# A hybrid decoder layer on one core: the Up projection's seven operands made ahead and kept in DRAM, and the last output projection moved to the channel mixer's entry

## The chip, the cores and the metric

The kernel runs on one core of one Trainium2 chip. The metric is the device time of one execution in microseconds (us). The engines are TensorE (PE in the rows, with PEld for its weight loads), VectorE (DVE), ScalarE (ACT) and GpSimd (POOL); SyncE (SP) issues nearly all transfers, in the order in which they stand in its program.

## The reference

One layer, 2048 tokens, model width 1024. The first half is the mixer, the second the channel mixer:

```python
h = modulate(x, norm_mix_g, sh_m, sc_m)
proj = h @ w_in
y = concat(gla_group(proj[:, :GLA_COLS]), rwkv7_group(proj[:, GLA_COLS:]))
x = x + gt_m * (y @ w_out)

h = modulate(x, norm_ffn_g, sh_f, sc_f)
u = h @ ffn_up                        # 1024 -> 2 * 2816
u = causal_conv3(u) + conv_b
gate, val = split(u, 2)
x = x + gt_f * ((silu(gate) * val) @ ffn_down)
out = rms_norm(x, final_g)

def modulate(x, g, shift, scale):     # rms_norm, then scale and shift
    return rms_norm(x, g) * (1 + scale) + shift
```

The RWKV group is a scan over tokens, so its blocks follow one another. All of it is float32.

## The kernel before

Tokens lie in 4 blocks of 512 (NB), activations as tiles of 128 features x 512 tokens, 8 tiles to a block (KT). Every large product of float32 is three matmuls of 128x128 by 128x512: operands are split into hi (a cast, ScalarE) and lo (a subtraction, VectorE or GpSimd), and hi*hi, lo*hi and hi*lo are added in PSUM.

Phase 1, the mixer, ends at about 1440 us. It runs GLA and RWKV in 16 quarters of a block (units; `rwkv_s` and what follows) and beside them a filler: the projections of the next block, and in the last block `spare()`, which is `stage_d` (the output projection) of blocks 0 to 2. `stage_d(b)` multiplies the mix of block b, read back from DRAM (`mixd`, mx), with w_out, eight output tiles ft, adds the residual, stores x2d[b] and makes the norm's rn2[b]. The RWKV part of a quarter ends in a chain: L738, L1017, the power L741 on GpSimd, L113, L1019, L1020, L1026, L1027 and the store of the mix, L1028.

Phase 2, the channel mixer, works on two halves e = 0, 1 of two blocks each. Up (class `Up`) treats two blocks x two halves of the 1024 features as a 2x2 matrix and uses seven products in place of eight (Strassen-Winograd): `Up(j, what)`, what = 1 to 7, is one of them for the pair of output tiles j (22 pairs), 12 matmuls (L1249 to L1251). The seven operands are b11, b21, b22 and the sums t1 to t4 of quarters of the modulated x; each has four k tiles, held as hi and lo for a whole half. `operands_a` makes b11 and b21: load x2d, multiply with the norm's row (L1144), add the shift (L1145, L1146). `operands_b` makes the other five, with `whole` (L1164) putting b11 and b21 together again from hi and lo. Weights are loaded into w_st (L1194), combined on GpSimd (L1227 to L1234) and split (L1124, L1125).

The hidden tiles go through the convolution and the gate (`conv`, `hidden`, in a background list bg, one piece per slot) and then, in groups of 2 or 4 pairs (kgroups), through Down: 16 slots a group, which load a partial sum acc from DRAM, add (L1306 to L1309) and store it.

Half 0 begins with the operands, made before `run`. Half 1 needs block 3, whose mix is the last that phase 1 stores. Its output projection `stage_d(NBLK - 1)` stands at the seam, with the operands of half 1, ahead of the last Down group of half 0 (d_begin, d_step, d_end). `run` goes through a list of slots; it asks for the loads of 6 slots ahead and prepares (splits) 3 ahead. The order within each engine's program is decided by a scheduler from these calls' order and priorities.

## Time and profile before

| | |
|---|---|
| three runs | 2959.83, 2950.89, 2960.01 us; median 2959.83 |
| profiled execution | 2950.25 us, its span 2948.5 us |
| TensorE, VectorE, ScalarE, GpSimd busy | 94%, 75%, 48%, 40% of the span |
| granted clock of TensorE, mean | 0.96 |

The span is the time from the first to the last instruction of the core; some 2 us lie around it. The busy shares are means over stages that differ: TensorE is near full over most of the span and has a few stretches with gaps. The profiled execution is at the lower edge of the three runs.

### The profile page before, as it was taken

To read this page: it belongs to the slowest core of one execution; us is meant where nothing else is said; L and a number is where in the kernel's file an instruction comes from. 1 tells how busy PE (TensorE), PEld (TensorE's weight loads), DVE (VectorE), ACT (ScalarE), POOL (GpSimd) and SP (SyncE) were. 2 spreads that over 40 slices of the span, in tenths; PEclk is the share of its full clock that TensorE was granted. 3 is DMA by queue.
4 is the path that set the end of the run, shared out by engine and by line. 5 is a ranking of instruction groups with operands and counts; after the bars stand their busy time and mean duration, and the time that the engine had idled before them with its cause. 6 is when DMAs were issued, how large, how long until landed. Compare 5 with 4: busy or idle time off the path is not lost.

```text
span 2948.5 us, 54765 instructions
## 1 busy us (share of the span) xinstructions
PE 2764.5 (94%) x20296; PEld 2231.9 (76%) x20296; DVE 2198.3 (75%) x4229; ACT 1407.2 (48%) x2909; POOL 1189.5 (40%) x1212
## 2 busy tenths in 40 slices
PE   6998899999999999899869999999998999999998
PEld 5777777877777777777658788888776788888887
DVE  7368787777877677888587775866879786685867
ACT  4555445445554565555444353533545453353443
POOL 5224232323222233334455463544537454363541
PEclk9999999999989999989979999999998999999999
DMA  8556544544333334533415334243465534425243
GB/s 282 173 166 190 159 122 136 151 143 120 113 112 101 109 115 148 148 101 105 151 53 164 116 104 153 91 138 125 147 200 171 193 101 139 129 97 161 85 132 109
DMA packets 316875, 401.95 MB, mean 136 GB/s; under 512 B 75584, under 2 KB 148544, under 8 KB 316608
## 3 DMA queue, kind: packets, MB, share of 16 engines
q1 hardware_dynamic: 316608, 398.45, 43.2%
q8 instruction: 160, 2.62, 0.4%
q14 instruction: 107, 0.88, 0.1%
HBM read 293.49 MB, written 104.86 MB: 135 GB/s over the span
## 4 chain that ended last, share of the span: by engine, by line
PE 60%; DVE 15%; DMA 7%; issue 3%; ACT 2%; POOL 2%; SPq 0%; DVEq 0%; POOLq 0%; ACTq 0%
PE g_bank L1251 9%; PE g_bank L1249 9%; PE g_bank L1250 9%; PE g_bank L1306 5%; PE g_bank L1308 5%; PE g_bank L1307 5%; PE g_bank L263 3%; PE g_bank L265 3%; PE g_bank L264 3%; DMA w_st<-in_ada_t 1%; DVE w_lo L182 1%; PE gl_bank L679 1%; DMA x_k<-in_x 1%; DMA ub<-x 1%; DVE gl_d L652 1%
## 5 line engine op out<-in xcount | busy, mean ns | idle before, releaser
L1249 PE MATMUL g_bank<-h_hi,w_hi 128*128 128x512 f32 x1232 | 488.7, 397 | 29.0 <-ACT h_hi L1124 12.4
L1251 PE MATMUL g_bank<-h_hi,w_lo 128*128 128x512 f32 x1232 | 481.7, 396 | 16.8 <-POOL w_lo L1125 12.3
L1250 PE MATMUL g_bank<-h_lo,w_hi 128*128 128x512 f32 x1232 | 487.7, 396 | 7.7 <-DVE h_lo L1125 4.7
L1124 ACT CAST w_hi<-w_st 128x512 fp32r<-128x512 f32 (+1 forms) x396 | 239.1, 609 | 465.6 <-PE g_bank L1307 342.6
L1309 DVE SCALAR_TENSOR_TENSOR acc<-g_bank,mod,acc 128x512 f32<-128x512 f32 (+1 forms) x200 | 144.9, 729 | 249.5 <-PE g_bank L1308 234.5
L1125 POOL TENSOR_TENSOR w_lo<-w_st,w_hi 128x512 fp32r<-128x512 f32 x154 | 221.5, 1439 | 229.2 <-ACT w_hi L1124 225.5
L263 PE MATMUL g_bank<-h_hi,w_hi 128*128 128x512 f32 x736 | 299.3, 408 | 5.2 <-ACT carry L320 3.8
L265 PE MATMUL g_bank<-h_hi,w_lo 128*128 128x512 f32 x736 | 297.4, 405 | 3.5 <-DVE w_lo L182 3.5
L1249 PEld LDWEIGHTS g_bank<-h_hi,w_hi 128*128 128x128 f32 x1232 | 235.5, 191 | 84.3 <-ACT h_hi L1124 14.7
L264 PE MATMUL g_bank<-h_lo,w_hi 128*128 128x512 f32 x736 | 295.9, 402 | 0.0
L1251 PEld LDWEIGHTS g_bank<-h_hi,w_lo 128*128 128x128 f32 x1232 | 235.7, 191 | 71.6 <-POOL w_lo L1125 17.8
L1250 PEld LDWEIGHTS g_bank<-h_lo,w_hi 128*128 128x128 f32 x1232 | 235.8, 191 | 58.9 <-DVE h_lo L1125 5.7
L1306 PE MATMUL g_bank<-hh,w_hi 128*128 128x512 f32 x640 | 251.5, 395 | 4.7 <-DVE acc L1309 4.6
L1308 PE MATMUL g_bank<-hh,w_lo 128*128 128x512 f32 x640 | 251.5, 395 | 0.0
L1307 PE MATMUL g_bank<-hl,w_hi 128*128 128x512 f32 x640 | 251.4, 395 | 0.0
L179 ACT CAST w_hi<-w_st 128x512 fp32r<-128x512 f32 x272 | 167.6, 619 | 118.8 <-PE g_bank L264 59.9
L182 POOL TENSOR_TENSOR w_lo<-w_st,w_hi 128x512 fp32r<-128x512 f32 x90 | 128.3, 1425 | 228.6 <-ACT w_hi L179 191.5
L1125 DVE TENSOR_TENSOR w_lo<-w_st,w_hi 128x512 fp32r<-128x512 f32 (+1 forms) x242 | 201.1, 831 | 19.4 <-ACT w_hi L1124 19.4
L182 DVE TENSOR_TENSOR w_lo<-w_st,w_hi 128x512 fp32r<-128x512 f32 x182 | 142.2, 782 | 63.6 <-ACT w_hi L179 52.9
L263 PEld LDWEIGHTS g_bank<-h_hi,w_hi 128*128 128x128 f32 x736 | 141.1, 192 | 37.5 <-ACT carry L320 4.8
L265 PEld LDWEIGHTS g_bank<-h_hi,w_lo 128*128 128x128 f32 x736 | 141.1, 192 | 36.1 <-DVE w_lo L182 5.2
L264 PEld LDWEIGHTS g_bank<-h_lo,w_hi 128*128 128x128 f32 x736 | 141.6, 192 | 28.7 <-issue 0.5
(344 smaller groups left out, 6382.1 us busy)
## 6 DMA issues: line engine op xcount, KB each, us to landing
acc<-acc SPq DMA_DIRECT2D x352, 256.0 KB, 3.1
w_st<-in_ffn_up SPq DMA_DIRECT2D x176, 256.0 KB, 3.0
w_st<-in_w_in SPq DMA_DIRECT2D x168, 256.0 KB, 3.0
proj<-ev SPq DMA_DIRECT2D x100, 256.0 KB, 3.0
w_st<-in_ffn_down SPq DMA_DIRECT2D x80, 256.0 KB, 2.7
w_st<-in_ada_t SPq DMA_DIRECT2D x64, 256.0 KB, 3.4
w_st<-in_w_out SPq DMA_DIRECT2D x64, 256.0 KB, 3.1
x_k<-in_x SPq DMA_DIRECT2D x48, 256.0 KB, 3.7
```

The source lines that it names most:

```text
L182: eng.tensor_tensor(out=lo[:, 0:w], in0=t[:, 0:w], in1=hi[:, 0:w].bitcast(F32), op=ALU.subtract)
L263: PE.matmul(out=ps, lhsT=wh, rhs=hi, start=k == 0, stop=False)
L264: PE.matmul(out=ps, lhsT=wh, rhs=lo, start=False, stop=False)
L265: PE.matmul(out=ps, lhsT=wl, rhs=hi, start=False, stop=k == KT - 1)
L1124: A.copy(out=hi, in_=t)
L1125: eng.tensor_tensor(out=lo, in0=t, in1=hi.bitcast(F32), op=ALU.subtract)
L1249: PE.matmul(out=ps, lhsT=wh[:, c], rhs=hi, start=first and k == 0, stop=False, skip_group_check=True)
L1250: PE.matmul(out=ps, lhsT=wh[:, c], rhs=lo, start=False, stop=False, skip_group_check=True)
L1251: PE.matmul(out=ps, lhsT=wl[:, c], rhs=hi, start=False, stop=last and k == 3, skip_group_check=True)
L1306: PE.matmul(out=ps, lhsT=wh, rhs=hh, start=j == 0, stop=False)
L1307: PE.matmul(out=ps, lhsT=wh, rhs=hl, start=False, stop=False)
L1308: PE.matmul(out=ps, lhsT=wl, rhs=hh, start=False, stop=j == n - 1)
```

## The change

The seven operands of a half are now made whole, in float32, and stored in DRAM (`opd`): `operand_rows` spreads the two norm rows, `operand_a` loads four tiles of x2d, modulates them and stores b11, b21 and b22, `operand_b` makes t1 to t4 of them in place on GpSimd and stores them. For half 0 this is done in phase 1, beside `stage_d(2)`, in memory of its own (pp); for half 1 in the background of half 0, after the Down groups that begin at 2, 6, 10 and 14. Where an operand is needed, `feed` loads it and splits it. The last output projection stands behind the first two units of half 0, its mix in the places of b22 and t4, whose feeds follow it. Both halves are one list of slots; the first two units of half 1 stand ahead of the last Down group of half 0, and the feeds of its operands beside j = 21 and that group.

```diff
+    pp = ph1.enter_context(tc.tile_pool(name="pp", bufs=1))
...
+    NAMES = ("b11", "b21", "t2", "t3", "t1", "b22", "t4")
+    opd = [{n_: [dram.tile([P, NB], F32, name=f"op_{e}_{n_}_{k}") for k in range(4)] for n_ in NAMES} for e in range(NBLK // 2)]
+    def operand_rows(e, r_of):
+        rbs = []
+        for i in range(2):
+            ps = pools["norm"]()
+            for t in range(4):
+                PE.matmul(out=ps[:, t * P:(t + 1) * P], lhsT=rn2[:, 2 * e + i, t:t + 1].broadcast_to([P, P]), rhs=ident, start=True, stop=True)
+            rb = r_of(i)
+            A.copy(out=rb, in_=ps)
+            rbs.append(rb)
+        return rbs
+    def operand_a(e, k, rbs, place):
+        t = {}
+        for n_, i, q in (("b11", 0, k), ("b12", 1, k), ("b22", 1, k + 4), ("b21", 0, k + 4)):
+            xk = place()
+            nc.sync.dma_start(out=xk, in_=x2d[2 * e + i][:, q, :])
+            V.scalar_tensor_tensor(out=xk, in0=xk, scalar=mod[:, 32 + q:33 + q], in1=rbs[i], op0=ALU.mult, op1=ALU.mult)
+            A.activation(out=xk, in_=xk, func=AF.Identity, bias=mod[:, 24 + q:25 + q])
+            if n_ in opd[e]:
+                nc.sync.dma_start(out=opd[e][n_][k], in_=xk)
+            t[n_] = xk
+        return t
+    def operand_b(e, k, t):
+        G.tensor_tensor(out=t["b12"], in0=t["b11"], in1=t["b12"], op=ALU.subtract)
+        G.tensor_tensor(out=t["b22"], in0=t["b12"], in1=t["b22"], op=ALU.add)
+        G.tensor_tensor(out=t["b11"], in0=t["b22"], in1=t["b11"], op=ALU.subtract)
+        G.tensor_tensor(out=t["b21"], in0=t["b22"], in1=t["b21"], op=ALU.subtract)
+        for n_, to in (("b12", "t1"), ("b22", "t2"), ("b11", "t3"), ("b21", "t4")):
+            nc.sync.dma_start(out=opd[e][to][k], in_=t[n_])
...
-            fin = yield from stage_d(b, hd.pop(b), pair=True, before=nxt, after=fin)
+            work = stage_d(b, hd.pop(b), pair=True, before=nxt, after=fin)
+            i = 0
+            while True:
+                try:
+                    next(work)
+                except StopIteration as end:
+                    fin = end.value
+                    break
+                if b == 2:
+                    if i == 0:
+                        rbs = operand_rows(0, lambda j: pp.tile([P, NB], F32, name="op_r", tag=f"r{j}", bufs=1))
+                    elif i < 5:
+                        t = operand_a(0, i - 1, rbs, lambda: pp.tile([P, NB], F32, name="op_x", tag="x", bufs=4))
+                        operand_b(0, i - 1, t)
...
-    def operands_a(b):
...
-    def operands_b(b, hs):
...
+    def feed(e, n_, k, hs):
+        t = ubt()[:, 0:NB]
+        nc.sync.dma_start(out=t, in_=opd[e][n_][k])
+        hi, lo = pair = hc(n_)
+        hs[n_].append(pair)
+        if n_ == "t2":
+            A.activation(out=hi, in_=t, func=AF.Copy, scale=-1.0)
+            V.scalar_tensor_tensor(out=lo, in0=t, scalar=-1.0, in1=hi.bitcast(F32), op0=ALU.mult, op1=ALU.subtract)
+        else:
             split(t, pair, either())
...
+    def feeds(e, names, hs):
+        return [lambda n_=n_, k=k: feed(e, n_, k, hs) for n_ in names for k in range(4)]
...
+    def out_begin():
+        places = iter(["b22"] * 4 + ["t4"] * 4)
+        pools["pair"] = lambda: hc(next(places))
+        out_begin.work = stage_d(NBLK - 1, prep_d(NBLK - 1), lp.tile([P, NB], F32, name="d_ss", tag="cv", bufs=4))
+    def out_step(i, more):
+        next(out_begin.work, None)
+        for p_ in more:
+            p_()
+    def out_end():
+        for _ in out_begin.work:
+            pass
+        bg.extend(feeds(0, ("b22", "t4"), hss[0]))
+    def next_rows():
+        next_rows.rbs = operand_rows(1, lambda j: lp.tile([P, NB], F32, name="op_r", tag="fs", bufs=HB))
+    def next_operand(k):
+        got = {}
+        bg.append(lambda: got.update(operand_a(1, k, next_rows.rbs, acct)))
+        bg.append(lambda: operand_b(1, k, got))
...
+            if e == 0 or j > 0:
+                U(j, 1)
+                U(j, 2)
+            if e == 0 and j == 0:
+                more = feeds(0, ("t2", "t3", "t1"), hss[0])
+                other(out_begin)
+                for i in range(KT):
+                    other(lambda i=i, m=more[i * 3 // 2:(i + 1) * 3 // 2]: out_step(i, m))
+                other(out_end)
             if j > 1 and group_of[j - 2] != group_of[j - 1]:
+                g = group_of[j - 2]
+                slots += down_slots(e, g, hids[e][g])
+                if e == 0 and g[0] == 0:
+                    other(next_rows)
+                elif e == 0 and g[0] <= 14:
+                    other(lambda k=(g[0] - 2) // 4: next_operand(k))
             if j > 0:
                 U(j - 1, 3)
...
+        if more_:
+            unit(1, 0, 1)
+            unit(1, 0, 2)
+            other(flush)
+            other(lambda: bg.extend(feeds(1, ("t2", "t3", "t1", "b22", "t4"), hss[1])))
+            other(lambda: sums[0].extend(lp.tile([P, NB], F32, name="x_ss", tag="fs", bufs=HB) for _ in range(HB)))
+            rest_ = down_slots(e, last, hids[e][last], sums[0])
+            for i, d_ in enumerate(rest_):
+                slots.append(d_)
+                other(lambda: None)
+            other(flush)
...
+    for p_ in feeds(0, ("b11", "b21"), hss[0]):
+        p_()
...
-    hs, pieces = operands_a(0)
-    for p_ in pieces:
-        p_()
-    for p_ in operands_b(1, hs):
-        p_()
```

The rows that follow are from the programs of the two kernels; the shape is that of the output. Lines of the changed kernel are shifted: its L1262 to L1264 are L1249 to L1251 of before, L1207 is L1194, L1030 is L1028, L743 is L741.

TensorE at the entry, before: the last quarter's small matmuls, and behind them the first units of the Up projection.

```order
L219 MATMUL g_bank<-ones_121,x_ss 128x1 x4
L1006 MATMUL rs_bank<-rw_t,rw_sv 64x64 x8
L1010 MATMUL rs_bank<-rw_rbk,rw_uv 64x64 x8
L232 MATMUL g_bank<-ident,rn_120 128x128 x8
L738 MATMUL rj_bank<-ct,rw_ysq 32x8 x16
L1249 MATMUL g_bank<-h_hi,w_hi 128x512 x2
L1250 MATMUL g_bank<-h_lo,w_hi 128x512
L1251 MATMUL g_bank<-h_hi,w_lo 128x512
```

Of the change, behind the same first two units: L263 to L265 are the last output projection.

```order
L1262 MATMUL g_bank<-h_hi,w_hi 128x512
L1263 MATMUL g_bank<-h_lo,w_hi 128x512
L1264 MATMUL g_bank<-h_hi,w_lo 128x512
L263 MATMUL g_bank<-h_hi,w_hi 128x512 x2
L264 MATMUL g_bank<-h_lo,w_hi 128x512
L265 MATMUL g_bank<-h_hi,w_lo 128x512
```

So between the second and the third product of Up there now stand the 192 matmuls of block 3's output projection, the first of them on mix tiles that are there, the later ones on those that the last store of the mix (L1030) brings.

SP at the entry, before: L1028 stores the mix of the last quarter, L1143 and L1171 load x2d for the operands.

```order
L1194 DMA w_st<-in_ffn_up 128x512 x4
L1143 DMA ub<-x_0_115 128x512 x2
L1171 DMA ub<-x_1_116 128x512 x3
L1194 DMA w_st<-in_ffn_up 128x512
L1028 DMA mix_114<-rw_yq 128x4x128
L1194 DMA w_st<-in_ffn_up 128x512
L1171 DMA ub<-x_1_116 128x512 x3
L1194 DMA w_st<-in_ffn_up 128x512
```

Of the change, from the store of the mix of the last quarter but one: op_x and op_b, op_t are tiles of the operands (the digit behind the letter is the k tile), L1060 and L1070 their stores, L1192 the loads of the feeds, L174 weights of the output projection.

```order
L1030 DMA mix_114<-rw_yq 128x4x128
L174 DMA w_st<-in_w_out 128x512 x5
L1060 DMA op_b_3_694<-op_x 128x512
L1060 DMA op_b_3_678<-op_x 128x512
L1070 DMA op_t_3_690<-op_x 128x512
L464 DMA x_2_117<-xr 128x512 x2
L174 DMA w_st<-in_w_out 128x512
L1070 DMA op_t_3_682<-op_x 128x512
L1070 DMA op_t_3_686<-op_x 128x512
L1070 DMA op_t_3_698<-op_x 128x512
L1192 DMA ub<-op_b_0_671 128x512
L1192 DMA ub<-op_b_1_672 128x512
```

The loads of the feeds stand behind the stores of all operands with k = 3, and the store of the last quarter's mix comes behind 13 of these loads.

GpSimd there, in the change: L1066 to L1068 are the last three differences of k = 3, L1240 and L1242 sums of Up weights, L743 the power of the last quarter.

```order
L1240 TENSOR_TENSOR w_st<-w_st 128x512
L1066 TENSOR_TENSOR op_x<-op_x 128x512
L1242 TENSOR_TENSOR w_st<-w_st 128x512
L1067 TENSOR_TENSOR op_x<-op_x 128x512
L1068 TENSOR_TENSOR op_x<-op_x 128x512
L743 TENSOR_TENSOR hn_rk<-hn_rk,mhalf 128x8
L1181 TENSOR_TENSOR h_lo<-ub,h_hi 128x512 x2
```

Before, no difference stood ahead of that power.

SP in the middle of half 0, in the change, after a Down group: L1338 and L1346 are loads and stores of acc, L1207 loads of weights of the Up projection.

```order
L1056 DMA acc<-x_2_117 128x512
L1070 DMA op_t_0_715<-acc 128x512
L1346 DMA acc_7_18305<-acc 128x512
L1060 DMA op_b_0_719<-acc 128x512
L1338 DMA acc<-acc_0_18290 128x512
L1060 DMA op_b_0_703<-acc 128x512
L1207 DMA w_st<-in_ffn_up 128x512
L1070 DMA op_t_0_707<-acc 128x512
L1338 DMA acc<-acc_0_18298 128x512
L1207 DMA w_st<-in_ffn_up 128x512
```

Before, only the rows of acc and the weights stood here.

## Rows read from the trace of the kernel before

**Rows 1.** Page: span; busy time, share and instructions of each engine:
```profile
span 2948.5 us, 54765 instructions
...
PE 2764.5 (94%) x20296; PEld 2231.9 (76%) x20296; DVE 2198.3 (75%) x4229; ACT 1407.2 (48%) x2909; POOL 1189.5 (40%) x1212
```
**Rows 2.** Windows; engines' busy us (x instructions), PEclk, DMA share, GB/s:
```profile
1460.00:1470.00 10.00, 9.35 (x29) 6.72 (x30) 9.87 (x16) 3.91 (x7) 6.67 (x4) 0.67 0.33 105
1500.00:1510.00 10.00, 0.98 (x3) 0.37 (x2) 9.48 (x10) 4.69 (x8) 6.18 (x6) 0.50 0.09 27
1440.80:1522.90 82.10, 45.52 (x240) 33.20 (x240) 66.32 (x82) 36.75 (x64) 50.69 (x37) 0.71 0.30 96
1850.00:1900.00 50.00, 50.00 (x221) 41.07 (x220) 47.03 (x54) 29.71 (x50) 35.02 (x34) 1.00 0.19 59
```
**Rows 3.** PE lines, 1440.8 to 1522.9: busy, mean ns, idle before:
```profile
L1249 PE MATMUL g_bank<-h_hi,w_hi 128*128 128x512 f32 x28 | 16.2, 585 | 25.2 <-ACT h_hi L1124 12.4 <-ACT h_hi L1145 8.5 <-ACT ub L1258 2.5
```
**Rows 4.** Waits of PE, 1440.8 to 1522.9: total us, times, longest:
```profile
PE g_bank L1249 <- ACT h_hi L1124: 12.4, 4, 5.7
PE g_bank L1249 <- ACT h_hi L1145: 8.5, 2, 5.2
```
**Rows 5.** PE timeline at the entry: start us, us:
```profile
1463.24 0.63 PE L1249 MATMUL g_bank<-h_hi,w_hi 128*128 128x512 f32 x1
1463.67 0.63 PE L1250 MATMUL g_bank<-h_lo,w_hi 128*128 128x512 f32 x1
```
**Rows 6.** Windows at the seam:
```profile
2100.00:2300.00 200.00, 180.99 (x776) 145.26 (x775) 176.20 (x214) 103.89 (x176) 107.98 (x83) 0.95 0.52 169
2305.00:2360.00 55.00, 49.94 (x197) 38.62 (x196) 40.00 (x55) 19.46 (x35) 25.34 (x21) 0.91 0.76 249
```
**Rows 7.** Lines of PE, 2100 to 2400:
```profile
L1251 PE MATMUL g_bank<-h_hi,w_lo 128*128 128x512 f32 x213 | 86.1, 407 | 11.7 <-POOL w_lo L1125 9.6 <-DVE w_lo L1125 2.0
...
L264 PE MATMUL g_bank<-h_lo,w_hi 128*128 128x512 f32 x64 | 24.9, 390 | 0.0
L232 PE MATMUL rj_bank<-ident,rn 128*128 128x128 f32 x24 | 3.2, 274 | 0.0
```
**Rows 8.** Waits of PE, 2100 to 2300 and 2305 to 2360:
```profile
PE g_bank L1251 <- POOL w_lo L1125: 9.1, 2, 8.3
...
PE g_bank L1306 <- DVE acc L1309: 3.7, 1, 3.7
```
**Rows 9.** Window at the end of phase 1:
```profile
1385.00:1445.00 60.00, 57.49 (x662) 46.09 (x660) 29.75 (x69) 25.17 (x58) 19.92 (x19) 1.00 0.45 144
```
**Rows 10.** Lines of POOL, 1385 to 1445:
```profile
L244 POOL TENSOR_TENSOR x_ss<-x_ss,x_sq 128x512 f32<-128x512 f32 x7 | 9.0, 1280 | 20.4 <-ACT x_sq L243 20.4
```
**Rows 11.** DMA issues: xcount, KB each, median us to landing:
```profile
mx<-mix SPq DMA_DIRECT2D x32, 256.0 KB, 3.2
...
mix<-rw_yq SPq DMA_DIRECT2D x16, 256.0 KB, 3.0
```
**Rows 12.** Timeline at the entry, POOL and SP:
```profile
1460.31 2.09 POOL L741 TENSOR_TENSOR hn_rk<-hn_rk,mhalf 128x8 f32<-128x8 f32 x1 [1.37 <-DVE hn_rk L1017]
...
1475.17 0.37 SPq L1028 DMA_DIRECT2D mix<-rw_yq  x1
```
**Rows 13.** Window with Down and Up matmuls in half 0:
```profile
1680.00:1730.00 50.00, 50.00 (x219) 40.66 (x218) 27.25 (x36) 15.84 (x26) 19.53 (x19) 1.00 0.57 173
```
**Rows 14.** Lines of DVE, 2100 to 2300:
```profile
L1125 DVE TENSOR_TENSOR h_lo<-ub,h_hi 128x512 fp32r<-128x512 f32 x14 | 12.8, 929 | 0.7 <-ACT h_hi L1124 0.7
...
L182 DVE TENSOR_TENSOR w_lo<-w_st,w_hi 128x512 fp32r<-128x512 f32 x11 | 9.8, 891 | 0.2 <-ACT w_hi L179 0.2
...
L1144 DVE SCALAR_TENSOR_TENSOR ub<-ub,mod,rbc 128x512 f32<-128x512 f32 x8 | 6.0, 745 | 1.4 <-DMA ub<-x 1.4
...
L1177 DVE TENSOR_TENSOR ub<-ub 128x512 f32<-128x512 f32 x4 | 2.8, 709 | 0.8 <-ACT ub L1173 0.8
```
**Rows 15.** Busiest window of the DMA queues:
```profile
1580.00:1590.00 10.00, 10.00 (x45) 8.09 (x44) 5.14 (x8) 2.44 (x4) 2.83 (x4) 1.00 0.94 318
```

More of the change, by code (lines that the diff above doesn't have):

```diff
@@ new lines, in hybrid_kernel, with other @@
+    hids, sums = {}, [[] for _ in range(NBLK // HB)]
+    last = kgroups[-1]
+    slots = []
+    def other(f):
+        slots.append(Other(f))
+    def out_begin():
[10 more added lines that the diff above has]
+        bg.extend(feeds(0, ("b22", "t4"), hss[0]))
@@ L1404, in stage_e @@
                 U(j - 1, 4)
+            if j == NH - 1:
+                step_early(3)
             U(j, 7)
+            if j == NH - 1:
+                step_early()
             U(j, 5)
[L1407 to L1442 removed]
@@ L1443, in stage_e @@
         U(NH - 1, 3)
         U(NH - 1, 4)
-        run(slots)
-        while bg:
-            bg_step()
-        while idle:
-            bg_step()
-        wplace, aplace = iter(["b11"] * 4 + ["b21"] * 4), iter(["t2"] * 4 + ["t3"] * 4)
-        ws, acc = [], [[], []]
-        for ft in range(KT):
-            pair = hc(next(wplace))
-            split(raw(ffn_down[ft][:, k0 * P:k1 * P]), pair, V)
-            ws.append(pair)
-            tag = next(aplace)
-            for i, s_ in enumerate(("hi", "lo")):
-                a_ = h1p.tile([P, NB], F32, name="acc", tag=f"{tag}_{s_}", bufs=4)
-                nc.sync.dma_start(out=a_, in_=accd[bs_[i]][ft])
-                acc[i].append(a_)
@@ L1475, in hybrid_kernel @@
+    for p_ in feeds(0, ("b11", "b21"), hss[0]):
         p_()
     pools["norm"] = lambda: bank("rj")
-    for e in range(NBLK // HB):
-        hs = stage_e(e, hs)
+    run(slots)
+    flush()
+    while idle:
+        bg_step()
+    e = NBLK // HB - 1
+    bs_ = range(e * HB, (e + 1) * HB)
+    k0, k1 = last
+    sums[e].extend(lp.tile([P, NB], F32, name="x_ss", tag="fs", bufs=HB) for _ in bs_)
+    hids, sums, hs = hids[e], sums[e], None
+    wplace, aplace = iter(["b11"] * 4 + ["b21"] * 4), iter(["t2"] * 4 + ["t3"] * 4)
```

135 lines of the change are left out of this document (41 added, 94 removed).

## Prediction

> **What bounds the kernel now.** I read the page first: TensorE is busy for 2764.5 of 2948.5 us [rows 1]. So a change off TensorE's path gains nothing, and one on it can gain at most the 184 us in which TensorE waits. Next I looked for where those are, with the windows of 10 us. Two stretches stand out, and the change touches both.
>
> *The entry of the channel mixer.* The pair of output projections that ends phase 1 is done at 1440.8; from 1523 TensorE runs without a gap. In the 82.1 us between it is busy for 45.5, at a granted clock of 0.71 [rows 2]. What it does there of use is 28 matmuls of each of L1249 to L1251, 84 in all [rows 3]. In steady state 221 such matmuls fill 50 us, 0.226 us each [rows 2]; so these 84 are worth 19.0 us. The other 63 us go to the 156 small matmuls of the RWKV tail and the norms (240 less 84) and, for the most part, to waiting. The waits say to whom: h_hi from ScalarE, 12.4 and 8.5 us [rows 4], that is the hi parts of Strassen operands. They are late because the whole chain that makes them (load, modulate, hi, lo, whole(), differences, split) stands on VectorE in this stretch and VectorE is full (9.48 of 10 us at 1500 to 1510, where TensorE has 0.98 and its granted clock is 0.50) [rows 2]. That is the lower of its two levels, 1.2 GHz of 2.4, and there consecutive matmuls start 0.43 us apart instead of 0.226 [rows 5].
>
> *The seam between the halves*, 2100 to 2400: VectorE is busy for 176.2 of 200 us, TensorE for 181 [rows 6]. In 300 us stand 638 matmuls of the Up projection, 288 of Down, 192 of the last output projection, 1118 in all [rows 7], worth 253 us; the small ones take some 7, of which the spreads L232 are 3.2 [rows 7]. So 40 us are lost here: about 10 of them in the Down group (0,2) of half 1, whose 197 matmuls are worth 45 of 55 us at a DMA share of 0.76 [rows 6] and where TensorE waits for acc [rows 8], and about 30 before it, where it waits for a w_lo that came 8.3 us late [rows 8] behind the operands' work.
>
> **The change at the entry.** Removed there: all of operands_a and operands_b. Added at the end of phase 1: per k tile 4 loads, 4 VectorE multiplies, 4 ScalarE biases, 4 GpSimd differences and 7 stores, 16 + 16 + 16 operations over four k tiles. Over the last 60 us of phase 1 GpSimd is busy for 19.9 and VectorE for 29.8 [rows 9], so 16 x 1.28 [rows 10] = 20 us of GpSimd and 16 x 0.75 (as L1144 has in [rows 14]) = 12 us of VectorE fit beside TensorE's projections, and I cost them at nothing there; if that cover failed, the 20 us of GpSimd would stand at the entry. Added at the entry: 28 feeds, each one load, one cast, one subtraction. And the last output projection, 192 matmuls, moves from the seam to this place.
>
> When can it start? The order has the last RWKV quarter, then the 24 matmuls of U(0,0,1) and U(0,0,2), then the projection on the first four k tiles of ft 0 and 1 (another 24), and only then what needs the last mix. SP has the feeds behind the stores of the k = 3 operands, and these wait for GpSimd, in whose order the last three differences of k = 3 stand just ahead of the power L743 of the last quarter. By rows: a k tile costs a load 3.2 [rows 11], multiply and bias at 0.75, four differences at 1.28 and a store 3.0, some 12 us; the x tiles of k = 3 are loaded when those of k = 2 are stored. I put the last difference at 1461, the first feed's landing at 1465, which is where the first matmuls of the units stood before (1463 [rows 5]). The quarter's tail: before, the power was at 1460.31 and the mix was stored at 1475.17, 14.9 us later [rows 12]. With VectorE freed of operands (9.87 of 10 us in 1460 to 1470 [rows 2]) I give it 12 us from 1461: 1473, and then store and load again, 3.0 + 3.2 [rows 11]: the fifth k tile's matmul at 1483 with what waits in SP between.
>
> From there TensorE has 168 matmuls of the projection and the ready operands t2, t3, t1 ahead of it. Counted at 1523: 48 + (1523 - 1483 - 3)/0.226 = 48 + 163 = 211 matmuls, against 84 before (the 3 us are for the restart at the lower clock). 127 x 0.226 = 28.7 us more work done. From it I take 3 us for b22 and t4, whose places hold the mix until the projection ends, so that their 8 feeds come after it. **Entry: -26 us.** Bounds: if the k = 3 chain is quick and the tail is not held, the start is at 1471: 264 matmuls, -38. If the k = 3 cycle is late by its whole 12 us and SP stands another 5 on the 14 transfers around it (0.82 us each, 256 KB at the 318 GB/s of [rows 15]), the start is at 1500: 136 matmuls, -9.
>
> **In half 0.** After four Down groups the operands of half 1 are made: each place adds 11 transfers, 4 VectorE multiplies, 4 biases, 4 differences. TensorE is at 50 of 50 us with VectorE at 47 [rows 2], so nothing is certain to hide them; but those rows are between Down groups, and the Down groups, where the places are, have VectorE at 27 of 50 [rows 13]. Bounds: nothing, and 4 places x 4 us of VectorE = 16 us. I take **+4 us**, near the lower end by the rows of the Down groups.
>
> **At the seam.** Removed from VectorE in 2100 to 2300: the output projection's and the operands' rows, from the 9.8 us of w_lo L182 to the 2.8 of L1177, eleven kinds with 72 us together, h_lo L1125 the largest [rows 14]. Added: 28 feeds, some 20 of them on VectorE at 0.93 us as h_lo has [rows 14], 19 us. The 192 matmuls leave. That removes the work behind which w_lo was late. What stays: the group (0,2) of half 1, 10 us. What is new: 20 feeds and the b22/t4 pair come in during the last Down group of half 0, which has 16 slots of 12 matmuls, 43 us, with VectorE also adding acc and squares; its 20 + 32 + 8 transfers of 256 KB are 15.7 MB, 49 us at the 318 GB/s of the busiest window [rows 15]. So transfers alone are a little over the matmuls: of the 30 us I take 14 as lost again there, half-way between the ends. **Seam: -16 us.** Bounds: -28 (2 of the 30 stay), -5 (the feeds come nearly as late as the operands did).
>
> Sum: 2950.25 - 26 + 4 - 16 = 2912 us against the profiled execution's own time (span 2948.5, 1.75 around it). The three runs have a median 9.6 us above that; I add a small part of it and say **2914**. A change under 0.3%, about 9 us, is none that a measurement can tell here.
>
> **A rule that speaks against it.** The change adds 112 transfers of 256 KB, 29.4 MB. At 318 GB/s [rows 15] they take 92 us if nothing hides them; in steady state 59 GB/s are moved [rows 2] and beside a Down group 173 [rows 13], so there is room for them, if not at each place. The Trainium skill, "DMA: Bandwidth & Descriptors", section "Where 436 GB/s comes from", puts the limit for a core's share of HBM at about 358 GB/s: by it an estimate of 82 us. The trace agrees so far: its busiest row, 318 GB/s, lies below that.
>
> **Rivals.**
> (a) *The operand chain holds the entry* (0.22): SP's order puts stores that wait for GpSimd ahead of the feeds, and the start is at 1500. Then the entry gives 9, the sum is 2929. For it: all loads and stores go through this one queue. Against it: GpSimd is idle for two thirds of the stretch in which it has to make k = 0 to 2 [rows 9].
> (b) *The seam gives nothing* (0.15): 20 feeds beside the last Down group in one queue cost what the operands did; 5 us instead of 16: 2923; with (a) 2940.
> (c) *Everything is at its good end* (0.15): -38, 0, -28: 2884.
> (d) *Slower* (0.07): in half 0 the weights of the Up projection (w_st) stand in SP's queue behind stores of b21 and t3 that wait for ScalarE and GpSimd. A unit's weights are asked for 6 slots ahead, 6 x 2.7 = 16 us of cover; a k tile's cycle of some 12 us plus its 11 transfers at 0.82 (9 us) is 21. If the cover is used up by acc traffic, each of four places loses up to 15 us: with (a) at the entry and the seam at 5, 2950 - 9 - 5 + 60 = 2996. It decides when a place loses more than 10 us (4 x 10 = the gain forecast). Against it: the rows of Down groups have TensorE at 50 of 50 at a DMA share of 0.57 [rows 13].
> (e) *Transfers are the bound* (0.02): all 92 us show, 2950 - 42 + 92 = 3000. Against it: the rates of [rows 2, 13].
> My forecast, a gain of 30 to 50, has 0.39.
>
> **How the numbers follow.** The likeliest is 2914; (c) and most of (a) and (b) are inside 2886 to 2944, and a little over 0.1 is left out on the upper side, under 0.1 below. Faster by over 0.3% holds in the forecast, (a), (b) and (c) except where (a) and (b) meet: 0.83. Within 0.3%: 0.08. Slower: 0.09, (d) and (e).
>
> **What would show it.** Right: L1249's idle at the entry (its waits for h_hi) falls from 21 to under 10 us; the output projection's matmuls run without gaps from about 1483; the granted clock of 1480 to 1520 is 1.00; VectorE at the seam falls from 88% to about 65%; the wait of 8.3 us for w_lo is gone; in 1600 to 2000 TensorE stays at 50 of 50. Wrong: a gap behind U(0,0,2) that lasts to 1500 and ends on the last mix; TensorE waiting for w_hi or w_lo around a Down group of half 0; a DMA share of 0.9 around 2230 with TensorE waiting for the feeds.

## The result, and the profile after

Five runs of each kernel on one chip: 2974.80 us (2972.22 to 2983.71) after the change, 2950.89 us (2946.09 to 2960.01) before it. The ratio of after to before is 1.0083, with a 95% interval of 1.0064 to 1.0102. The changed kernel is 0.8% slower. I had forecast 2914 us, faster; the range ended at 2944.

The page of the changed kernel (its profiled execution took 2979.16 us):

```profile
span 2977.3 us, 55039 instructions
...
PE 2778.9 (93%) x20296; PEld 2244.9 (75%) x20296; DVE 2163.9 (73%) x4191; ACT 1409.3 (47%) x2925; POOL 1202.0 (40%) x1234
```

Against [rows 1], VectorE has 34 us less to do and the span is 28.8 us longer. Work was removed; the time went into standing. Windows show where. The columns are those of [rows 2]; the first two rows lie in half 0, each just behind a place where operands of half 1 are made, then come the entry and the seam:

```profile
1750.00:1800.00 50.00, 41.73 (x161) 32.59 (x161) 40.25 (x44) 25.52 (x44) 30.22 (x29) 0.90 0.42 131
2000.00:2050.00 50.00, 43.14 (x179) 34.07 (x178) 29.88 (x34) 18.31 (x31) 26.02 (x23) 0.97 0.53 172
...
1440.80:1522.90 82.10, 57.59 (x357) 46.02 (x358) 52.99 (x80) 40.45 (x71) 42.08 (x33) 0.77 0.81 273
1500.00:1510.00 10.00, 10.00 (x38) 8.03 (x38) 8.30 (x11) 6.53 (x11) 4.86 (x4) 0.82 1.00 350
2100.00:2300.00 200.00, 182.01 (x752) 144.31 (x751) 138.09 (x179) 85.04 (x146) 90.70 (x76) 0.95 0.57 183
```

At the entry TensorE starts 357 matmuls where it started 240, and at 1500 to 1510 it is busy for 10.00 us where it had 0.98 [rows 2]: the change does there what it says. At the seam VectorE falls from 176.20 of 200 us [rows 6] to 138.09. But in half 0, where [rows 2] had 221 matmuls in 50 us, there are now stretches with 161 and 179.

**A curve of progress.** To add this up I counted TensorE's large matmuls (128x128 by 128x512, 8720 in each kernel) in order of start and noted when the n-th starts. At one n both kernels have started equally many; those of the last output projection (192) come between n = 2841 and 3045 after the change and between 5505 and 5720 before it, and count as any others. The table is the time in a run's profiled execution less the time at the same n before. Up to n = 2200 every engine has the same program in all of them (the first difference is a load of op_x in SP's, at 1163 us), yet the executions differ there, after the change by 5.2 us (1110.3 and 1115.5); that is no effect of the change, so this lag (last column) is taken off each curve. (With it, the last row is 29.1 us; the spans differ by 28.8.) Three of the four places in which half 1's operands are made lie between n = 3800 and 5330, the fourth between 5500 and 5580, inside the stretch in which the kernel before has its seam.

```
us later than before, from n = 2200
n                          3050    3800    5330    8720 (end)  lag at 2200
after                     -14.2   -12.3   +24.4   +23.9       +5.2
e1 half 1 not made        -15.1   -12.3   -13.4   -30.6       +9.1
e2 half 1 not computed    -16.8   -14.7   -12.5   -26.9       +1.8
e3 other ring             -13.1   -10.1    -1.6   -11.5       +4.7
e4 half 0 not made        -32.0   -29.9    +3.7    +1.2      +12.7
e5 other ring             -14.4   -12.6    -7.7   -22.0       +2.9
e6 other ring             -13.5   -10.4    -4.5   -16.4       +7.1
e7 as e3, earlier         -14.0   -12.2    -6.4   -14.4       +3.7
e8 as e3, k = 3 late       -5.6    -3.9    +2.0    -8.5       +5.3
e9 as e5, norm late       -16.0   -11.9    -9.4   -19.3       +8.2
e10 as e9, earlier        -21.8   -15.0   -12.8   -25.0       +8.2
e11 as e9, on GpSimd      -22.4   -14.8   -13.7   -27.0       +4.5
e12 as e11, order         -22.0   -11.0    -8.4   -23.0       -0.1
```

How far can one such row be read? e3, e5 and e6 came out as one and the same program (see there). Their rows lie 1.3 us apart at n = 3050 (3.7 with those of the changed kernel, e1 and e2, which are the same program up to there too), lose 8.5, 4.9 and 5.9 us over the three places, and end 10.5 us apart. Differences of that size between two rows say nothing.

Row "after" is the whole account. The entry gains 14.2 us where I had 26. Then 1.9 are lost up to n = 3800, in e1 and e4 as well (2.8 and 2.1). The three places lose 36.7: from n = 3900 to 4040 13.3, from 4440 to 4510 10.4, from 4950 to 5030 8.6, the rest between. From n = 5330 on 0.5 is gained, although the fourth place loses 9.4 there, where e1 and e5 gain 2.8; so that place costs 12.2, and without it the seam gives 12.7, where I had 16.

### The profile page after: what moved, and what is told of

The parts are those of the page before. It is cut to its first block, busy times and chain, and to the rows that moved or that the text cites. A ratio compares the mean times of both kernels' runs of the same rounds, so it can differ in the third digit from the quotient of the medians.

```text
span 2977.3 us, 55039 instructions
## 1 busy us (share of the span) xinstructions
PE 2778.9 (93%) x20296; PEld 2244.9 (75%) x20296; DVE 2163.9 (73%) x4191; ACT 1409.3 (47%) x2925; POOL 1202.0 (40%) x1234
## 4 chain that ended last, share of the span: by engine, by line
PE 56%; DVE 14%; DMA 10%; issue 3%; ACT 3%; POOL 2%; SPq 1%; DVEq 0%; POOLq 0%; ACTq 0%
PE g_bank L1264 8%; PE g_bank L1262 8%; PE g_bank L1263 8%; PE g_bank L1319 5%; PE g_bank L1321 4%; PE g_bank L1320 4%; DMA acc<-acc 2%; PE g_bank L263 2%; PE g_bank L265 2%; PE g_bank L264 2%; DMA acc<-x 1%; DMA w_st<-in_ada_t 1%; PE gl_bank L681 1%; DVE w_lo L182 1%; DVE rw_pr L884 1%
## 5 line engine op out<-in xcount | busy, mean ns | idle before, releaser
L1262 PE MATMUL g_bank<-h_hi,w_hi 128*128 128x512 f32 x1232 | 488.6, 397 | 20.6 <-ACT ub L1271 10.7
L1264 PE MATMUL g_bank<-h_hi,w_lo 128*128 128x512 f32 x1232 | 484.1, 397 | 24.5 <-DVE w_lo L1181 17.5
L1322 DVE SCALAR_TENSOR_TENSOR acc<-g_bank,mod,acc 128x512 f32<-128x512 f32 (+1 forms) x200 | 144.5, 728 | 229.7 <-PE g_bank L1321 211.9
L263 PE MATMUL g_bank<-h_hi,w_hi 128*128 128x512 f32 x736 | 300.5, 410 | 7.1 <-ACT carry L320 3.9
L265 PE MATMUL g_bank<-h_hi,w_lo 128*128 128x512 f32 x736 | 298.6, 406 | 0.0
L1264 PEld LDWEIGHTS g_bank<-h_hi,w_lo 128*128 128x128 f32 x1232 | 235.5, 191 | 81.7 <-DVE w_lo L1181 21.9
L1262 PEld LDWEIGHTS g_bank<-h_hi,w_hi 128*128 128x128 f32 x1232 | 236.1, 192 | 75.6 <-ACT ub L1271 14.1
L263 PEld LDWEIGHTS g_bank<-h_hi,w_hi 128*128 128x128 f32 x736 | 142.0, 193 | 39.5 <-ACT carry L320 4.9
L265 PEld LDWEIGHTS g_bank<-h_hi,w_lo 128*128 128x128 f32 x736 | 142.0, 193 | 30.9 <-issue 0.2
```

The costliest lines, as they stand in the source:

```text
L263: PE.matmul(out=ps, lhsT=wh, rhs=hi, start=k == 0, stop=False)
L265: PE.matmul(out=ps, lhsT=wl, rhs=hi, start=False, stop=k == KT - 1)
L1262: PE.matmul(out=ps, lhsT=wh[:, c], rhs=hi, start=first and k == 0, stop=False, skip_group_check=True)
L1264: PE.matmul(out=ps, lhsT=wl[:, c], rhs=hi, start=False, stop=last and k == 3, skip_group_check=True)
```

## The experiments

My first theory: tiles of the new background work (L1056 to L1070) come from acct(), the ring of 5 buffers that Down uses for its partial sums, so a load of x2d can't be issued before a store of acc has landed; the engines, which run in order, stand on the tile. The rivals: the stores in SP's queue, with w_st behind them (rival (d)); the transfers as such (rival (e)); the arithmetic.

**e1, half 1's operands not made.** 2928.61 us, ratio 0.9894 [0.9870, 0.9919].

```diff
-        nc.sync.dma_start(out=t, in_=opd[e][n_][k])
+        nc.sync.dma_start(out=t, in_=opd[0][n_][k])
...
-                elif e == 0 and g[0] <= 14:
+                elif False:
```

> Leaves out the making of half 1's operands in half 0 (its feeds load those of half 0). Theory A (the four places in half 0 cost the time: VectorE and ScalarE stand in order on tiles whose loads wait for a buffer of the acc ring) and theory B (the 44 transfers and SP's queue cost it) both expect that the jumps of some 10 us at each of the four places in the progress of TensorE's large matmuls vanish: 35 to 45 us less, a time of 2930 to 2942. If the single list of slots or the feeds cost the time, it stays at 2970 to 2978.

From n = 3800 to 5330 it loses nothing (-1.1), and from there it gains 17.2. So the whole loss in half 0 comes from making half 1's operands there, and without it the change would gain 1.1%; that is an upper end, since e1 leaves needed work out.

**e2, loads and stores of half 1's operands without the arithmetic.** Same places, same queue, same ring, same bytes. 2931.26 us, ratio 0.9911 [0.9881, 0.9942].

```diff
+            if e == 0:
                 V.scalar_tensor_tensor(out=xk, in0=xk, ...)
                 A.activation(out=xk, in_=xk, ...)
...
+        if e == 0:
             G.tensor_tensor(out=t["b12"], ...)      # and the other three
```

> Half 1's operands in half 0 without their arithmetic: the 4 loads and 7 stores at each place stay, on the same ring of 5 buffers; the multiplies, biases and differences are left out. Theory A expects most of the loss gone, since nothing on VectorE or ScalarE waits for these tiles any more: 2938 to 2952. Theory B expects the loss to stay, since the queue and the bytes do: 2962 to 2976.

The three places cost 2.2 us in place of 36.7 (the time is even below the range that theory A gave), with TensorE at 49.40 of 50 us in the window that had 41.73:

```profile
1750.00:1800.00 50.00, 49.40 (x218) 40.59 (x217) 45.87 (x53) 28.07 (x48) 34.20 (x31) 1.00 0.32 107
```

So the transfers and their place in SP's queue cost next to nothing by themselves: what is lost needs an engine that touches the tile. (SP's own wait for the ring is shorter in e2, 6.5 us in 3 waits of L1056 at 1600 to 2100 where it was 25.3 in 9.) Four multiplies of 0.75 us are 3 us a place, not 10, so it is the standing that counts. That is what VectorE's waits in half 0 say. After (total us, times, longest):

```profile
DVE acc L1322 <- PE g_bank L1321: 95.9, 61, 2.1
DVE acc L1057 <- DMA acc<-x: 52.4, 16, 9.2
```

ScalarE has the same 52.4 us behind it, and SP, which issues the loads, waits for Down's stores at the first place (1740 to 1766). The waits of ScalarE, then of SP:

```profile
ACT acc L1058 <- DVE acc L1057: 52.4, 15, 10.3
```

```profile
SPq L1056 <- DMA acc<-acc: 8.8, 3, 3.9
```

Sixteen waits are four places times four tiles. e2 leaves out the work of VectorE, ScalarE and GpSimd at once, so it doesn't say how much of the loss is whose. The timeline of VectorE at the first place (start, us; in brackets the idle time and what ended it) shows what is queued behind:

```profile
1747.87 0.95 DVE L1057 SCALAR_TENSOR_TENSOR acc<-acc,mod,op_r 128x512 f32<-128x512 f32 x1 [8.37 <-DMA acc<-x]
1748.73 0.74 DVE L1322 SCALAR_TENSOR_TENSOR acc<-g_bank,mod,acc 128x512 f32<-128x512 f32 x1
1751.67 0.75 DVE L1057 SCALAR_TENSOR_TENSOR acc<-acc,mod,op_r 128x512 f32<-128x512 f32 x1 [2.19 <-DMA acc<-x]
1754.30 0.78 DVE L1057 SCALAR_TENSOR_TENSOR acc<-acc,mod,op_r 128x512 f32<-128x512 f32 x1 [1.88 <-DMA acc<-x]
1755.01 0.74 DVE L1322 SCALAR_TENSOR_TENSOR acc<-g_bank,mod,acc 128x512 f32<-128x512 f32 x1
1755.67 0.68 DVE L1181 TENSOR_TENSOR w_lo<-w_st,w_hi 128x512 fp32r<-128x512 f32 x1
1757.93 1.67 DVE L1057 SCALAR_TENSOR_TENSOR acc<-acc,mod,op_r 128x512 f32<-128x512 f32 x1 [1.59 <-DMA acc<-x]
```

For 8.37 us before 1747.87 VectorE does nothing; the Down addition L1322, then a w_lo of the next Up, then the convolution stand behind it. TensorE meets this as waits for w_lo and for ub, ScalarE's copies out of PSUM, which stand behind its L1058. Its waits in half 0, 1600 to 2100, after:

```profile
PE g_bank L1264 <- DVE w_lo L1181: 12.4, 6, 2.9
PE g_bank L1262 <- ACT ub L1271: 8.8, 6, 3.2
PE g_bank L1264 <- POOL w_lo L1181: 3.7, 4, 1.9
PE g_bank L1262 <- ACT w_hi L1180: 1.3, 1, 1.3
```

That is 26 us of plain waiting, where the trace before has one row of 1.5 in this stretch; the granted clock of 0.90 at 1750 to 1800 is the rest that I can see.

**e3 and e5, operand tiles from another ring.** In the source, e5 changes that alone (4 buffers of "cv", the convolution's ring); e3 also asks for the work after the fourth slot of the Down group in place of behind it. e5: 2939.10 us, 0.9930 [0.9898, 0.9961]. e3: 2936.50 us, 0.9931 [0.9911, 0.9950].

```diff
-        bg.append(lambda: got.update(operand_a(1, k, next_rows.rbs, acct)))
+        bg.append(lambda: got.update(operand_a(1, k, next_rows.rbs, lambda: lp.tile([P, NB], F32, name="op_x", tag="cv", bufs=4))))
```

> All work done, but half 1's operand tiles lie in the ring of the convolution (cv, 4 buffers, free during a Down group) in place of the acc ring, and are made after the fourth slot of the Down group in place of after its last. Theory A expects the waits of L1057 on loads to fall under 2 us each and the places to cost 0 to 3 us each: 2936 to 2950. Theory B expects no gain, the transfers now meeting those of acc head on: 2968 to 2990.

> The ring alone: half 1's operand tiles lie in cv (4 buffers) in place of the acc ring, their place after the Down group is unchanged. Theory A in its narrow form (a buffer of the acc ring comes free only when a Down store has landed) expects L1057's waits to fall from 52 to under 25 us and half of the 38 us at the four places to go: 2945 to 2958. If the place behind the Down group is what costs (the convolution of the next pair needs VectorE and cv then), it stays above 2962.

One word of the source decides: the three places cost 4.9 us in e5 in place of 36.7, and the kernel is faster than before. TensorE's waits in the same 500 us of half 0 are down to

```profile
PE g_bank L1264 <- POOL w_lo L1181: 4.9, 4, 1.9
PE g_bank L1319 <- DVE acc L1322: 0.6, 1, 0.6
```

But the word changes more than the ring. The scheduler now gives the work another place: at the first Down group the multiplies stand ahead of its first additions, some 55 us earlier than after the change, and don't wait. VectorE in e5:

```profile
1691.47 0.75 DVE L1057 SCALAR_TENSOR_TENSOR op_x<-op_x,mod,op_r 128x512 f32<-128x512 f32 x1
...
1698.79 1.40 DVE L1057 SCALAR_TENSOR_TENSOR op_x<-op_x,mod,op_r 128x512 f32<-128x512 f32 x2
```

In e3 they are at the same place (1695.75 the first): the order of the instructions on VectorE, ScalarE, GpSimd and SP, and that of the large matmuls, is the same in both traces, whatever the source asked for. So e3 is e5's program once more, and no test of the place. What these two show is the new ring together with the place that comes with it. That the acc ring makes the loads late is read from SP's waits above; a run with "cv" behind the Down group, or with the acc ring ahead of it, would tell the two apart, and there is none.

Rival (d) falls in its own form: in e5, SP still waits for the stores' ScalarE results (7.5 us in 8 waits at 1600 to 2100, after the change 3.8 in 5), with the weights behind, and nearly nothing is lost. VectorE's additions now wait for Down's own loads (L1322 on acc: 25.6 us in 10 waits in e5, 42.0 in 16 in e3, none before), and TensorE hardly feels it.

**e6, the same work on "cv", asked for in 12 pieces,** one after each Down slot from the third: 2938.61 us, 0.9928 [0.9897, 0.9960].

```diff
+                    for i_, d_ in enumerate(ds):
+                        slots.append(d_)
+                        if i_ >= 2 and tiles:
+                            other(tiles.pop(0))
```

> As e3, but the pieces are spread over the Down group, one after each slot from the third on: four loads, then four multiplies with biases and stores, then four differences with stores. Theory A expects that the 42 us in which e3's additions (L1322) waited for acc become fewer, since the loads stand ahead of their use and between those of acc: 8 to 12 us less than e3 in half 0, 2924 to 2934. Theory B' (the 11 transfers cost in any order) expects e3's time, 2934 to 2943.

The 2924 to 2934 of theory A did not come. But the scheduler gave e6 the order of e3 and e5 again: it is the same program a third time, and whether spreading the work would help was not tried.

**e4, half 0's operands not made in phase 1.** 2959.64 us, 1.0014 [0.9996, 1.0032].

```diff
-                    if i == 0:
-                        rbs = operand_rows(0, ...)
-                    elif i < 5:
-                        t = operand_a(0, i - 1, rbs, ...)
-                        operand_b(0, i - 1, t)
+                    pass
```

> Leaves out the making of half 0's operands in phase 1 (its feeds load tiles of x2d). Theory C (at the end of phase 1 VectorE stands on the loads of k = 2 and 3, and the last residual tile, the sum of squares and with it TensorE's L219 and the last RWKV quarter come late): L219's wait of 8.8 us goes, the first Up matmul comes 15 to 25 us earlier than at 1482, and the time falls by 12 to 22 us to 2952 to 2963. Rival D (the entry is set by the last quarter's own chain and by the store and load of its mix): less than 5 us, 2969 to 2977.

The entry gains 32.0 us in place of 14.2: making half 0's operands, which I had hidden beside phase 1, costs 18 us here. As theory C had it, L219 doesn't wait and the first Up matmul starts at 1465.67; which of the two links holds the tail is not shown by that, since e4 takes all the work away. The loss in half 0 stays (33.6 us from n = 3800 to 5330); it is a second, independent one.

Where do the 18 us go? In the changed kernel's timeline of TensorE at the entry, the last projections of phase 1 end at 1454, and then:

```profile
1455.76 0.69 PE L1012 MATMUL rs_bank<-rw_rbk,rw_uv 128*64 128x64 f32 x16
1465.21 1.87 PE L219 MATMUL g_bank<-ones,x_ss 128*128 128x1 f32 x8 [8.76 <-POOL x_ss L244]
1469.21 1.12 PE L974 MATMUL rs_bank<-rw_sv,rw_t 128*64 128x64 f32 x16 [2.13 <-ACT rw_yq L1013]
...
1482.35 0.80 PE L1262 MATMUL g_bank<-h_hi,w_hi 128*128 128x512 f32 x1 [2.94 <-ACT h_hi L1180]
...
1494.92 0.73 PE L263 MATMUL g_bank<-h_hi,w_hi 128*128 128x512 f32 x2 [3.08 <-ACT h_hi L418]
```

The first Up matmul (L1262, L1249 before) starts at 1482.35 where the kernel before has its first at 1454.61, and the projection runs on without larger gaps from 1498, not 1483. (5.2 us of such differences are the lag at n = 2200.) What is late is the RWKV tail. L974, which begins the last quarter, waits for ScalarE's L1013, which waits to overwrite a buffer whose store to the mix is still to land:

```profile
1468.79 0.37 ACT L1013 COPY rw_yq<-rs_bank 128x256 f32<-128x256 f32 x1 [3.49 <-DMA mix<-rw_yq]
```

That store is late because VectorE's L1029, which makes it, stands behind the multiplies of k = 2 and 3, and these wait for loads that wait for the stores of the k tile before (4 buffers). VectorE, then SP:

```profile
1455.58 0.75 DVE L1057 SCALAR_TENSOR_TENSOR op_x<-op_x,mod,op_r 128x512 f32<-128x512 f32 x1 [2.01 <-DMA op_x<-x]
...
1462.36 0.68 DVE L1029 TENSOR_TENSOR rw_yq<-rj_bank,rw_yq 128x512 f32<-128x512 f32 x1
```

```profile
1463.07 0.37 SPq L1030 DMA_DIRECT2D mix<-rw_yq  x1
...
1492.14 0.37 SPq L1030 DMA_DIRECT2D mix<-rw_yq  x1
```

The last mix is stored at 1492.14, 17 us later than before [rows 12], 11.8 without the lag. Two things can be the bound: the norm of `stage_d(2)` (L219, 8.76 us, ahead of L974 on TensorE), or the store chain. The next experiments try to take the one or the other away.

**e7 and e8.** e7 is e3 with the phase 1 work one step earlier and 5 buffers: 2935.16 us, 0.9927 [0.9900, 0.9953]. e8 is e3 with only k = 0 to 2 made in phase 1 and k = 3 behind it: 2954.71 us, 0.9995 [0.9979, 1.0011].

```diff
-                    elif i < 5:
-                        t = operand_a(0, i - 1, rbs, ... bufs=4))
-                        operand_b(0, i - 1, t)
+                    if i < 4:
+                        t = operand_a(0, i, rbs, ... bufs=5))
+                        operand_b(0, i, t)
```

```diff
-                    elif i < 5:
+                    elif i < 4:
...
+    next_rows.rbs = operand_rows(0, ...)
+    operand_b(0, 3, operand_a(0, 3, next_rows.rbs, ...))
```

> As e3, and half 0's operands in phase 1 begin one step of the output projection earlier, with 5 buffers in place of 4. Theory C (loads of k = 2 and 3 late for want of buffers, VectorE standing on them ahead of the last residual tile) expects L219's wait of 8 to 9 us to fall under 3 and the entry to gain 8 to 15 us on e3: 2922 to 2930. If the ring isn't the cause, L219's wait stays and the time is e3's, 2934 to 2943.

> As e3, and the operands of half 0's last k tile are made after phase 1, behind the feeds' first loads, so that nothing of k = 3 stands ahead of the residual's last tiles. Theory C expects L219's wait under 2 us and the last RWKV quarter 8 to 10 us earlier; but the first units then need k = 3 itself: a gain of 0 to 10 us on e3, 2926 to 2938. If the tail doesn't move, C is wrong.

Both missed. e7 moves the entry by 1 us only (-14.0 against -13.1), and L219 still waits 7.3 us. e8 is worse: less work in phase 1 doesn't free L219, and the first Up matmul stands on the operands. The waits of TensorE in e8, 1400 to 1560:

```profile
PE g_bank L1262 <- ACT h_hi L1180: 11.4, 1, 11.4
PE g_bank L219 <- POOL x_ss L244: 7.8, 1, 7.8
```

**e9 and e10, the norm of block 2 out of the way.** e9 is e5 with the sum of squares stored and the norm made later, with `next_rows`, so that L219 no longer stands ahead of L974. 2935.77 us, 0.9934 [0.9912, 0.9956]. e10 adds e7's earlier start: 2943.73 us, 0.9962 [0.9944, 0.9980].

```diff
-        fin()
+        nc.sync.dma_start(out=ssd, in_=ss2)
...
+        t = lp.tile([P, NB], F32, name="op_x", tag="cv", bufs=4)
+        nc.sync.dma_start(out=t, in_=ssd)
+        rstd_tok(rn2[:, 2], sum_tok(t))
```

> As e5, and the norm of block 2 (L219 on x_ss, needed only for half 1) is taken out of phase 1: its sum of squares is stored and read back in half 0. Theory C1 (L219, standing in TensorE's order ahead of the last RWKV quarter, holds it for the 8.8 us of its wait) expects the quarter's first matmul L974 6 to 9 us earlier and the same in the end: 2924 to 2933 where e5 has 2939. Theory C2 (the quarter also waits for the store of the previous quarter's mix, late because VectorE stands on operand loads ahead of L1029) expects L974 to wait for ScalarE's L1013 in its place: 0 to 3 us.

> As e9, with half 0's operands one step earlier and 5 buffers, as in e7. C1 expects e9's time. C2 expects little on e9 too unless the fifth buffer moves L1029 (1462 before): 0 to 4 us.

The timeline of TensorE in e9:

```profile
1470.70 1.12 PE L974 MATMUL rs_bank<-rw_sv,rw_t 128*64 128x64 f32 x16 [11.98 <-ACT rw_yq L1013]
```

With L219 gone, L974 starts at 1470.70 (1467.08 in e5) and waits 11.98 us for L1013. e9 lagged by 8.2 us at n = 2200 and e5 by 2.9; without that L974 is 1.7 us earlier, where C1 expected 6 to 9. The norm was cover, not cause; the store chain is the bound, and the entry gains 1.6 us over e5, no more than such rows differ by. e10's entry is another 5.8 us better in its trace (-21.8), but its median is not: the intervals of the ratios overlap, and I draw nothing from it.

**e11, the multiply of half 0's operands on GpSimd** with the scale in ScalarE's bias step, so that VectorE has nothing of this chain, on top of e9: 2932.32 us, 0.9929 [0.9906, 0.9953].

```diff
+            if e == 0:
+                G.tensor_tensor(out=xk, in0=xk, in1=rbs[i], op=ALU.mult)
+                A.activation(out=xk, in_=xk, func=AF.Identity, scale=mod[:, 32 + q:33 + q], bias=...)
```

> As e9, and in phase 1 the multiply of half 0's operands is done on GpSimd (a product with the norm row; the scale goes into ScalarE's activation), so that VectorE no longer stands on operand loads. C2 expects L1029 of the last quarter but one 4 to 6 us earlier, the quarter's L974 too, and 4 to 10 us on e9; but GpSimd, which then has eight operations per k tile, may hold L743 and the feeds. C1 alone expects e9's time.

The last store of the mix moves to 1475.57, as early as in [rows 12], 16.6 us before that of the changed kernel:

```profile
1475.57 0.37 SPq L1030 DMA_DIRECT2D mix<-rw_yq  x1
```

In e9 it is at 1493.05. Without the lags of the traces (e11 4.5, e9 8.2) that is 13.8 us earlier, and the same 1471.1 as in e4, where this work isn't done at all (1483.77, lag 12.7). So VectorE's order was what held the tail. But of the 13.8 us only 6.4 arrive at n = 3050 (-22.4 against -16.0 in e9), and the median is 3.4 us under e9's, with intervals that overlap (expected: 4 to 10). Now the first Up matmul (L1269 here) waits for its operands, whose feeds stand behind the k = 3 stores. Waits of TensorE, 1440 to 1520:

```profile
PE g_bank L1269 <- ACT h_hi L1187: 10.2, 1, 10.2
PE rs_bank L974 <- ACT rw_yq L1013: 8.3, 1, 8.3
```

**e12, the projection ahead of U(0,0,1) and U(0,0,2),** on top of e11: 2930.27 us, 0.9912 [0.9895, 0.9930].

```diff
-            if e == 0 or j > 0:
-                U(j, 1)
-                U(j, 2)
             if e == 0 and j == 0:
                 ...                       # the last output projection
+            if e == 0 or j > 0:
+                U(j, 1)
+                U(j, 2)
```

> As e11, and block 3's output projection stands ahead of the first two Up units in place of behind them. In e11 the last mix was stored 16 us earlier than in the changed kernel, but the first Up unit then waited 10.2 us for operands (feeds behind the stores of k = 3), and the projection stood behind it. If that order is what is left at the entry, the projection's matmuls run from about 1478 and the entry gains 5 to 10 us on e11: 2921 to 2928. If the feeds only move the gap behind the projection, or its weights are late, 0 to 2 us: 2929 to 2935.

The wait of 10.2 us is replaced by one of 3.6, but at n = 3050 the entry stands where e11 had it (-22.0 and -22.4); 2930.27 lies in the second range, that of 0 to 2 us:

```profile
PE rs_bank L974 <- ACT rw_yq L1013: 8.5, 1, 8.5
PE rj_bank L113 <- ACT hn_rx L745: 5.6, 1, 5.6
PE g_bank L264 <- DVE h_lo L419: 3.6, 1, 3.6
```

From there to n = 3800 it gives 11.0 us of that back, so at the end it is where e5 and e11 are. It does all the work and beats both kernels; against e3, e5 to e7, e9 and e11 the intervals overlap, so I can't say that it is the best of them. Why the lead of the entry melts between n = 3050 and 3800 (by 1.9 us after the change, 7.6 in e11, 11.0 in e12) is open. In e12 TensorE waits 9.7 us at 1500 to 1760, for parts of the weights and for ub, and VectorE is busy for 18.9 to 19.1 of each 20 us from 1620 to 1680; that VectorE's work of half 0 is the next bound fits this, but no run tried it.

## Why the prediction was wrong

**The step that failed is the cost of half 0: "+4 us, near the lower end by the rows of the Down groups".** I costed the added operations by what the engines do, and put them beside Down groups because VectorE is at 27 of 50 us there [rows 13]. That is right as far as it goes: with tiles of another ring, ahead of the Down group, they cost 4.9 us for three places (e5). What I never asked is where acct() takes its tiles from. Each multiply needs a load, each load a buffer that Down is still using, and VectorE and ScalarE take such an instruction in order, with Down's additions and the weights' lo parts behind it. 13.3, 10.4, 8.6 and 12.2 us at the four places are 44.5 us (the bound that I gave was 16). e2 shows that it needs an engine that touches the tile; e5 shows that it goes with the ring, or with the place behind the Down group that the scheduler gives the work on this ring. These two were not told apart.

**Rival (d)** had the sign, the place and nearly the size ("a place loses more than 10 us"), but not the mechanism: it had the weights late in SP's queue behind stores. e2 has the loads and stores in SP's queue and loses 2.2 us, e5 has the stores' waits there and loses 4.9. I gave it 0.07; the price of 15 us a place was right to think about, and one look at the tile's tag would have raised the chance. **Rival (e)**, transfers as the bound, is refuted by the same two runs.

**The entry term was mis-sized: -26 forecast, -14.2 measured,** inside the bounds of -9 to -38, and by what rival (a) says: the operand chain holds the entry, and the projection runs from 1498 (rival (a): 1500). The steps that failed are "I put the last difference at 1461, the first feed's landing at 1465" and "12 us of VectorE fit beside TensorE's projections". GpSimd in the changed kernel, with the last three differences (L1066 to L1068) and the power of the last quarter (L743):

```profile
1473.29 1.27 POOL L1066 TENSOR_TENSOR op_x<-op_x 128x512 f32<-128x512 f32 x1
...
1475.74 1.45 POOL L1067 TENSOR_TENSOR op_x<-op_x 128x512 f32<-128x512 f32 x1
1477.15 1.45 POOL L1068 TENSOR_TENSOR op_x<-op_x 128x512 f32<-128x512 f32 x1
1479.73 1.65 POOL L743 TENSOR_TENSOR hn_rk<-hn_rk,mhalf 128x8 f32<-128x8 f32 x1 [1.13 <-DVE hn_rk L1019]
```

The last difference ends at 1478.6, 17 us later than I put it (12 without the lag), and the feeds come behind its store. Rival (a) had that, and in e11 it is the wait of 10.2 us. (Nor do the first matmuls of the units stand at 1463 before, as I wrote: those are later ones, the first is at 1454.61.) The power stands right behind the differences too, but it waits 1.13 us more for VectorE's L1019: the tail itself came late, by the waits of VectorE's multiplies for loads, with L1029 behind them (e11 against e9: the last mix is stored 13.8 us earlier without the lags). That link rival (a) had not. It is the same mistake as in half 0: 12 us of work fit, but a wait on a transfer isn't work and fits nowhere. e4 puts its price at 18 us at the entry; e11 gets back 8 of these from e5, and e12 no more.

**The seam came out near its size:** -16 forecast, -12.7 measured when the fourth place is set aside, -14.3 in e5 and -17.2 in e1 from n = 5330. VectorE fell from 88% to 69% (I had said about 65%), and the wait of 8.3 us for w_lo [rows 8] is gone; the longest single ones there are now 5.2 us for hh from ScalarE and 4.3 for acc. But the 14 us that I took as lost again have no ground left: they came from transfers at 318 GB/s as the busiest window [rows 15], and that isn't the busiest. At the 396 of a window near the start (last section) I would have put the 15.7 MB at 40 us, under the 43 of the matmuls. That half of the 30 us stayed is luck as far as the runs show; what holds it was not tried.

Sum of what was measured from n = 2200: -14.2 + 1.9 + 36.7 + 12.2 - 12.7 = +23.9 us; the forecast's was -38. Of the 62 us between them the four places make up 44.9 (48.9 measured against 4), the entry 11.8, the stretch behind the entry 1.9 and the seam 3.3.

**The signs that I had named.** TensorE's waits for h_hi of Up at the entry fell from 21 us [rows 4] to 2.9: right. The projection was to run without gaps from about 1483, and it does from 1498: wrong. The granted clock of 1480 to 1520 was to be 1.00 and is 0.83: wrong, since the projection began later. "In 1600 to 2000 TensorE stays at 50 of 50": wrong, and "TensorE waiting for w_hi or w_lo around a Down group of half 0" is what came, as the list of what would make the prediction wrong had it.

## What to carry to other kernels

When background work is put beside a tuned loop, look first at which ring its tiles come from: a load into a ring that the loop itself uses waits for the loop's stores, and the first in-order engine that touches the tile then stands with the loop's own work behind it (52.4 us here for 12 us of arithmetic). Changing that one tag, which also moved the work ahead of the loop, turned 0.8% slower into 0.7% faster. Look, too, at the order that comes out and not only at the source: three variants with the work asked for at three places were one program. Work that fits by busy shares may still not fit by its waits; and a wait that is named on the path (L219 here) can be cover for a longer one behind it, so try it before you mend it.
